# One run of row products a layer instead of four, in the gated recurrence of a decoder trunk

## The chip, the cores and the metric

The kernel runs on one core of a Trainium2 chip. The core has five engines with a queue each: TensorE (PE in the profile; PEld is its loading of weights), VectorE (DVE), ScalarE (ACT), GpSimd (POOL) and SyncE (SP). Data lie in SBUF, and matmuls write to PSUM banks of 128 x 512 numbers. The metric is the device time of one execution in microseconds. Three runs of the kernel before took 386.99, 387.08 and 389.15 us; the median is 387.08.

## What is computed

Two layers of a decoder trunk on 256 positions of width 1024. Each layer normalises x, projects it to 10 groups of 512 columns, feeds three branches (block-sparse attention, a gated recurrence and cross-attention to a memory of 256 tokens), gates their outputs, projects them back and adds x. The change touches the recurrence alone, in the reference:

```python
def step(state, inp):                      # chunks of 64 positions, 4 heads, key and value width 128
    qc, lfc, kc, vc = inp
    A = jnp.cumsum(lfc, axis=2)
    diff = A[:, :, :, None, :] - A[:, :, None, :, :]
    decay = jnp.exp(jnp.where(causal[:, :, None], diff, -jnp.inf))
    scores = jnp.einsum('bhtd,bhtsd,bhsd->bhts', qc, decay, kc)
    o = (jnp.einsum('bhts,bhsv->bhtv', scores, vc)
         + jnp.einsum('bhtd,bhdv->bhtv', qc * jnp.exp(A), state))
    A_end = A[:, :, -1:, :]
    state = (jnp.exp(A_end[:, :, 0, :])[..., None] * state
             + jnp.einsum('bhsd,bhsv->bhdv', kc * jnp.exp(A_end - A), vc))
    return state, o
```

A score of positions t and s is thus the sum over 128 key dimensions of q(t), k(s) and the product of the forget gates between s and t.

## The kernel before

**Projections.** Weights come in chunks of 128 x 1024 (60 chunks a layer, the counter is `st["c"]`). Each chunk is loaded by DMA into `wr`, rounded by ACT to a high half `wh` (L213) and DVE subtracts to get the low half `wl` (L227). PE multiplies high by high, high by low and low by high (L275, products of 128 x 512, some of 128 x 256). Three buffers each hold `wh` and `wl`. After some of these products the emitting code calls `slot`, which makes further chunks (`h_to`, `l_to`) and lets every active generator go one step.

**Generators.** The branches are Python generators (`g_hgrn` is the recurrence). A `yield 2` lets two steps pass, and so places the generator's next instructions further on among the projections. `room(what, n)` waits, while the program is emitted, until n tiles of a kind are free in a bookkeeping (`held`, `room_of`); `rel` gives one back. Side tiles (`sd`) are four PSUM banks.

**Order.** `schedule_with_timeline_sim=True` (L1499) lets a planner order the instructions of each engine along a simulated timeline. `keep_in_program_order` pins an instruction (`mm_row`, L278, does it for the row products), and `in_turn` writes an order out by hand. Hand-written orders cover the chunks up to 13 of layer 1 (L1318 to L1333) and, in both layers, those from 36 on (L1304 to L1316, L1335 to L1344); the recurrence lies between them, in chunks 16 to 31.

**The recurrence.** With keys on partitions, Q, K and F (forget gates) are 128 x 1024 tiles, one column a position and head. The decay between positions is built level by level, so that every score inside a block of 32 positions is a product of a Q column that carries some gates and a K column that carries others:

- level 1 (pairs): Q carries F (L896), then a row run (L899), then the pair's gate product hT1 (L901), hQ2 (L904) and K times F in place (L907);
- levels m = 2 and m = 8 (L911 to L954): Q columns (L919, L920), a row run (L924), gate products, the next Q tile (L947 to L949), and K of three of four groups times a gate, in place (L950);
- the carry at 32 (`carry`, L866) writes hQb and hKb, and a last run (L961 to L973) multiplies K and Q between blocks of 32 and of 64;
- the carry at 64 (L975) works in place, and hKb times hQb of whole heads follows (L991).

A row run (`row`, L880) is 32 products, eight by four, each with a 128 x 32 piece of K as weights and 48 columns of Q, into four 32-partition strips of one side tile. Each shows in the trace as two matmuls, so a run has 64. The masked copies (`keep`, L889, on DVE at L892) take from the side tile the parts that belong to this level into the block-diagonal tile hSd; two follow the first run and three each the next two. hSd and the last run's side tile are then copied into hST (L978, L983, on ACT). Much later the products of hST with the values follow (L1008).

Since K is changed in place, the K product of a level waits for the row run that reads it.

Of the kernel before, what the change touches and what calls it, by code (L numbers as in the profile page):

```python
# [12 lines left out]
F32 = mybir.dt.float32  # L13
# [5 lines left out]
OP = mybir.AluOpType  # L19
# [26 lines left out]
def hymba_kernel(ctx: ExitStack, tc: tile.TileContext, x, mem, mem_t, positions, w_in, w_out, w_mem_kv,  # L46
                 gains, moba_g, out):
    nc = tc.nc
# [15 lines left out]
    def room(what, n=1):  # L64
        while held[what] + n > room_of[what]:
            yield
# [14 lines left out]
    def rel(what="sd", n=1):  # L81
        held[what] -= n
# [696 lines left out]
    def pairs(a, n):  # L779
        return a.rearrange("p (n m) -> p n m", m=n)  # L780
# [76 lines left out]
    def g_hgrn(l):  # L857
# [8 lines left out]
        def carry(m, Tm, src, dst=None):  # L866
            (Qv, Kv), (Qo, Ko) = ([halves(a, m) for a in p] for p in (src, dst or src))
            n = 1024 // (2 * m)
            Tv = Tm.rearrange("p (n two) -> p n two", two=2)
            nc.vector.tensor_tensor(Qo[:, :, 1], Qv[:, :, 1], Tv[:, :, 0:1].to_broadcast([128, n, m]), op=OP.mult)  # L870
            nc.vector.tensor_tensor(Ko[:, :, 0], Kv[:, :, 0], Tv[:, :, 1:2].to_broadcast([128, n, m]), op=OP.mult)
            if dst is not None:
                nc.scalar.copy(Qo[:, :, 0], Qv[:, :, 0])
                nc.scalar.copy(Ko[:, :, 1], Kv[:, :, 1])
            if m < 64:
                T2 = sb.tile([128, n], F32, name=f"hT{m}", tag=f"hT{m}", bufs=1)
                nc.vector.tensor_tensor(T2, Tv[:, :, 0], Tv[:, :, 1], op=OP.mult)
                return T2

        def row(q, m):  # L880
            g = side_tile()
            for i in range(8):
                for j in range(4):
                    c = i * 4 + j
                    mm_row(g[j * 32:j * 32 + 32, i * 48:i * 48 + 48].rearrange("p (n m) -> p n m", m=m),
                           K[:, c * 32:c * 32 + 32], q(c))
            return g[:, :384].rearrange("p (a n m) -> p a n m", a=8, m=m)

        def keep(g, j, n, lo, hi):  # L889
            def part(a):  # L890
                return a.rearrange("p a (n m) -> p a n m", m=n)[:, :, :, lo:hi]
            nc.vector.copy_predicated(part(hSd), part(mk[:, j][:, None, :].to_broadcast([128, 8, 32])), g)  # L892


        F2, K2 = pairs(F, 2), pairs(K, 2)
        nc.vector.tensor_tensor(Q[:, :, 2], Q[:, :, 1], F2[:, :, 1], op=OP.mult)  # L896
        yield 2
        yield from room("sd")
        g = row(lambda c: Q[:, c * 16:c * 16 + 16], 3)  # L899
        Tm = sb.tile([128, 512], F32, name="hT1", tag="hT1", bufs=1)  # L900
        nc.vector.tensor_tensor(Tm, F2[:, :, 0], F2[:, :, 1], op=OP.mult)  # L901
        yield 2
# [1 line left out]
        nc.vector.tensor_tensor(n4[:, :, 0:4], Q[:, :, 0:3:2].rearrange("p (g a) i -> p g a i", a=4),  # L904
                                F2[:, :, 0].rearrange("p (g a) -> p g a", a=4)[:, :, :, None]
                                .to_broadcast([128, 128, 4, 2]), op=OP.mult)
        nc.vector.tensor_tensor(K2[:, :, 0], K2[:, :, 0], F2[:, :, 1], op=OP.mult)  # L907
        keep(g[:, :, :, 0:2], 0, 2, 0, 2)
        keep(g[:, :, :, 2:3], 1, 2, 1, 2)
        rel()  # L910
        for m in (2, 8):  # L911
            n = 256 // m
            q, T4, K4 = n4, pairs(Tm, 4), K.rearrange("p (g a i) -> p g a i", a=4, i=m)

            def by(j, w, k=None):
                return T4[:, :, j:j + w, None].to_broadcast([128, n, w, m]) if k is None else \
                    T4[:, :, j:j + 1, None].to_broadcast([128, n, k, m])
            yield
            nc.vector.tensor_tensor(q[:, :, 4:6], q[:, :, 2:4], by(1, 2), op=OP.mult)  # L919
            nc.vector.tensor_tensor(q[:, :, 6:7], q[:, :, 5:6], by(1, 1), op=OP.mult)  # L920
            yield 2
            yield from room("sd")
            b = 8 // m
            g = row(lambda c: q[:, c * b:c * b + b, 1:7].rearrange("p g a i -> p g (a i)") if b > 1  # L924
                    else q[:, c, 1:7].rearrange("p a i -> p (a i)")[:, None, :], 6 * m)
            nc.vector.tensor_tensor(T4[:, :, 2], T4[:, :, 2], T4[:, :, 3], op=OP.mult)
            nc.vector.tensor_tensor(T4[:, :, 1], T4[:, :, 1], T4[:, :, 2], op=OP.mult)
            Tn = sb.tile([128, n], F32, name=f"hT{m}", tag=f"hT{m}", bufs=1)
            nc.vector.tensor_tensor(Tn, T4[:, :, 0], T4[:, :, 1], op=OP.mult)
            yield 2  # L930
            if m == 2:
                n4 = sb.tile([128, 32, 7, 8], F32, name="hQ3", tag="PTh", bufs=1)

                def to(c, w):
                    return n4[:, :, 0:4].rearrange("p g a (c i) -> p g a c i", i=m)[:, :, :, c:c + w]

                def split(a):
                    return a.rearrange("p (g b) a i -> p g b a i", b=4)
            else:
                n4 = sb.tile([128, 1024], F32, name="hQ", tag="hq0", bufs=1)  # L940

                def to(c, w):
                    return n4.rearrange("p (g c i) -> p g c i", c=4, i=m)[:, :, c:c + w]

                def split(a):
                    return a
            nc.scalar.copy(to(0, 1), split(q[:, :, 0:1]))  # L947
            nc.vector.tensor_tensor(to(1, 1), split(q[:, :, 1:2]), split(by(0, 1)), op=OP.mult)
            nc.vector.tensor_tensor(to(2, 2), split(q[:, :, 4:7:2]), split(by(0, 1, 2)), op=OP.mult)  # L949
            nc.vector.tensor_tensor(K4[:, :, 0:3], K4[:, :, 0:3], by(1, 3), op=OP.mult)  # L950
            for k, (lo, hi, at) in enumerate(((1, 4, 0), (2, 4, 3), (3, 4, 5))):
                keep(g[:, :, :, at * m:(at + hi - lo) * m], (2 if m == 2 else 5) + k, 4 * m, lo * m, hi * m)
            rel()
            Tm = Tn  # L954
        base = n4, K
        other = [sb.tile([128, 1024], F32, name=n, tag=t, bufs=1) for n, t in (("hQb", "PTl"), ("hKb", "PTh"))]
        yield
        T2 = carry(32, Tm, base, other)
        yield 2
        yield from room("sd")  # L960
        g = side_tile()  # L961
        for a in range(0, 8, 2):
            for q in (0, 64):
# [4 lines left out]
        for a in range(0, 8, 2):  # L968
            for b in range(2):
                for q in (0, 32):  # L970
                    c = (a + b) * 128
                    mm_row(g[b * 64 + q:b * 64 + q + 32, 128 + a * 32:128 + a * 32 + 64],
                           other[1][:, c + q:c + q + 32], other[0][:, c + 64:c + 128])  # L973
        yield 2
        carry(64, T2, other)  # L975
        S2 = St.rearrange("p (a b) s -> p a b s", b=2)
        for q in range(0, 128, 32):
            nc.scalar.copy(St[q:q + 32, :, q:q + 32], hSd[q:q + 32])  # L978
# [10 lines left out]
        g = side_tile()  # L989
        for h in range(4):  # L990
            mm(g[:, h * 128:(h + 1) * 128], K4[:, h, 0:128], Q4[:, h, 128:256], True, True)  # L991
        rel("PTh")
        rel("PTl")
        xc = sb.tile([128, 512], F32, name="hX", tag="hX", bufs=1)
        nc.scalar.copy(xc, g)
        rel()
# [506 lines left out]
```

## Time and profile before

| | |
|---|---|
| median of three runs | 387.08 us |
| profiled execution | 387.04 us, span 385.3 us |
| granted PE clock | 0.999 |
| PE, PEld busy | 99%, 83% |
| DVE, ACT, POOL busy | 84%, 65%, 23% |
| matmuls that are row products or the last run's (L279, hQ with hK, hQb with hKb) | 448 + 64 |

How to read what is quoted. The page gives the busy time of each engine, and the chain of work that ended last, followed back from the last instruction. In the chain in order of time a line is start, length and the pieces merged into it. A list of waits has the engine and line that waited, who released it, the total, how often and the longest. A row of a timeline is start, length, engine, line, operation, output <- inputs, shape and count, with the idle time of the engine ahead of it and its releaser in brackets. Ends of matmuls are modelled and overlap, so their starts are what to go by. Tile names lose their trailing numbers: hQ stands for hQ1, hQ2, hQ3 and hQ.

### The profile page before, as it was taken

To read this page: it belongs to the slowest core of one execution; us is meant where nothing else is said; L and a number is where in the kernel's file an instruction comes from. 1 tells how busy PE (TensorE), PEld (TensorE's weight loads), DVE (VectorE), ACT (ScalarE), POOL (GpSimd) and SP (SyncE) were. 2 spreads that over 40 slices of the span, in tenths; PEclk is the share of its full clock that TensorE was granted. 3 is DMA by queue.
4 is the path that set the end of the run, shared out by engine and by line. 5 is a ranking of instruction groups with operands and counts; after the bars stand their busy time and mean duration, and the time that the engine had idled before them with its cause. 6 is when DMAs were issued, how large, how long until landed. Compare 5 with 4: busy or idle time off the path is not lost.

```text
span 385.3 us, 6801 instructions
## 1 busy us (share of the span) xinstructions
PE 379.6 (99%) x2447; PEld 318.9 (83%) x2447; DVE 322.9 (84%) x631; ACT 249.4 (65%) x422; POOL 89.4 (23%) x135
## 2 busy tenths in 40 slices
PE   7999999999999999999999999999999999999996
PEld 5888888788888888888888888888888888888885
DVE  4789799999679999967596989899698699798763
ACT  4988855567769749654366866445765985794540
POOL 3004400643202523220031030014062063134000
PEclk9999999999999999999999999999999999999999
DMA  7985595438534889875559667736756189898612
GB/s 255 421 323 186 177 315 198 149 128 277 215 109 159 273 272 354 317 259 169 162 168 299 200 210 236 255 111 184 253 193 194 54 277 269 318 325 264 202 39 109
DMA packets 26577, 85.53 MB, mean 222 GB/s; under 512 B 3632, under 2 KB 6064, under 8 KB 26544
## 3 DMA queue, kind: packets, MB, share of 16 engines
q1 hardware_dynamic: 22304, 71.31, 55.4%
q0 software_dynamic: 3952, 13.64, 11.3%
q8 instruction: 19, 0.31, 0.3%
q10 hardware_dynamic: 288, 0.15, 0.1%
q14 instruction: 14, 0.11, 0.1%
HBM read 75.13 MB, written 9.96 MB: 221 GB/s over the span
## 4 chain that ended last, share of the span: by engine, by line
PE 97%; DMA 1%; DVE 0%; SPq 0%; ACT 0%; issue 0%; DVEq 0%
PE acc L275 58%; PE acc L1361 17%; PE acc L310 11%; PE sd L275 5%; PE sd L279 4%; DMA wr<-in_w_mem_kv_dram 1%; PE sd L1071 0%; PE sd L1205 0%; PE sd L490 0%; PE acc L279 0%; PE sd L545 0%; SPq L177 0%; ACT wh L217 0%; DVE xs L1415 0%; DVE xs L1422 0%
## 5 line engine op out<-in xcount | busy, mean ns | idle before, releaser
L213 ACT CAST wh<-wr 128x1024 fp32r<-128x1024 f32 x96 | 100.8, 1051 | 58.0 <-PE acc L275 38.8
L227 DVE TENSOR_TENSOR wl<-wr,wh 128x1024 fp32r<-128x1024 f32 x96 | 117.1, 1222 | 22.6 <-ACT wh L213 20.4
L275 PE MATMUL acc<-wh,hT 128*128 128x512 f32 x384 | 123.1, 394 | 0.0
L275 PEld LDWEIGHTS acc<-wh,hT 128*128 128x128 f32 x384 | 71.5, 188 | 15.0 <-issue 0.7
L275 PE MATMUL acc<-wl,hT 128*128 128x512 f32 x192 | 75.6, 394 | 0.0
L275 PE MATMUL acc<-hT,wh 128*128 128x512 f32 x256 | 63.9, 392 | 0.0
L275 PEld LDWEIGHTS acc<-hT,wh 128*128 128x128 f32 x256 | 46.5, 189 | 8.5
L275 PEld LDWEIGHTS acc<-wl,hT 128*128 128x128 f32 x192 | 36.1, 188 | 7.3
L217 ACT ACTIVATE wh<-wr,gT 128x1024 fp32r<-128x1024 f32 (+1 forms) x29 | 28.9, 1011 | 13.1 <-DMA wr<-in_w_mem_kv_dram 5.9
L1361 PE MATMUL acc<-wl,yh 128*128 128x512 f32 (+1 forms) x96 | 37.2, 387 | 0.0
L1361 PE MATMUL acc<-wh,yl 128*128 128x512 f32 (+1 forms) x96 | 37.1, 387 | 0.0
L275 PEld LDWEIGHTS acc<-hT,wl 128*128 128x128 f32 x256 | 34.8, 190 | 2.2
L231 DVE SCALAR_TENSOR_TENSOR wl<-wr,gT,wh 128x1024 fp32r<-128x1024 f32 (+1 forms) x29 | 31.1, 1096 | 6.1 <-ACT wh L217 6.1
L275 PE MATMUL acc<-hT,wl 128*128 128x256 f32 x256 | 35.7, 282 | 0.0
L1361 PE MATMUL acc<-wh,yh 128*128 128x512 f32 (+1 forms) x96 | 30.6, 390 | 0.0
L310 PE MATMUL acc<-wh,mTh 128*128 128x512 f32 x64 | 25.4, 400 | 1.0 <-ACT wh L217 0.7
L1036 POOL TENSOR_TENSOR rka<-msa,pw 128x8 f32<-128x8 f32 x4 | 12.1, 3022 | 59.2 <-DVE msa L1035 59.2
L310 PE MATMUL acc<-wh,mTl 128*128 128x512 f32 x64 | 24.8, 390 | 0.0
L1116 ACT ACTIVATE P<-P,nba,rq 128x128 f32<-128x128 f32 (+1 forms) x32 | 17.1, 536 | 7.0 <-DVE nba L1110 7.0
L1361 PEld LDWEIGHTS acc<-wh,yl 128*128 128x128 f32 x96 | 18.0, 188 | 3.7
L1361 PEld LDWEIGHTS acc<-wl,yh 128*128 128x128 f32 x96 | 18.0, 188 | 3.6
L1361 PEld LDWEIGHTS acc<-wh,yh 128*128 128x128 f32 x96 | 17.7, 188 | 3.6 <-issue 0.3
(233 smaller groups left out, 591.3 us busy)
## 6 DMA issues: line engine op xcount, KB each, us to landing
wr<-in_w_in_dram SPq DMA_DIRECT2D x80, 512.0 KB, 4.2
wr<-in_w_out_dram SPq DMA_DIRECT2D x24, 512.0 KB, 4.9
wr<-in_w_mem_kv_dram SPq DMA_DIRECT2D x15, 512.0 KB, 5.2
there<-blk POOLq DMA_DIRECT2D x7, 512.0 KB, 4.8
there<-blk POOLq DMA_DIRECT2D x4, 768.0 KB, 6.3
PT<-there POOLq DMA_DIRECT2D x16, 192.0 KB, 5.7
there<-blk SPq DMA_DIRECT2D x4, 512.0 KB, 2.9
P<-there POOLq DMA_DIRECT2D x16, 128.0 KB, 3.9
```

Source lines behind the costliest of these rows:

```text
L213: N["wh", i] = nc.scalar.copy(whs[i], raws[i])
L217: N["wh", i] = nc.scalar.activation(whs[i][:, sl], raws[i][:, sl], AF.Copy, scale=gT[:, g:g + 1])
L227: N["wl", i] = nc.vector.tensor_tensor(wls[i], raws[i], whs[i].bitcast(F32), op=OP.subtract)
L231: ins = nc.vector.scalar_tensor_tensor(wls[i][:, sl], in0=raws[i][:, sl], scalar=gT[:, g:g + 1], in1=whs[i][:, sl].bitcast(F32), op0=OP.mu ...
L275: nc.tensor.matmul(o, lhsT=a, rhs=b, start=s, stop=e)
L279: tc.keep_in_program_order(nc.tensor.matmul(o, lhsT=a, rhs=b, start=s, stop=e))
L310: N["kv", i, g, t, j] = nc.tensor.matmul(acc[g][t], lhsT=x[:, c, ts], rhs=y, start=c == 0 and j == 0, stop=c == 7 and j == 2)
L1036: nc.gpsimd.tensor_tensor(r[:, t8], ms[:, t8], pw[:, :8], op=OP.pow)
L1116: N["exp", u, c] = nc.scalar.activation(P[:, i, kc[t]], P[:, i, kc[t]], AF.Exp, bias=nb[:, c:c + 1], scale=rq[:, r:r + 1], accum_out=sm[:, ...
L1361: ins = nc.tensor.matmul(a, lhsT=y, rhs=wt[:, cs], start=n == (0 if to is None else nk - 2) and j == 0, stop=n == nk - 1 and j == 2)
```

## The change

The row products of levels 1, 2 and 8 are no longer issued when their Q and K columns are ready. Each level puts its K tile, a function that cuts its Q columns and a width on a list, and all three runs are issued ahead of the last run, once four side tiles are free, so that 128 products stand together. For that, what they read has to stay until then: K after levels 1, 2 and 8 is written to a tile of its own each time (hK1, hK2, hK8, in buffers of tiles that are idle there), with the part that isn't multiplied copied by ACT; hQ3 moves to a buffer of P, and hQb and hKb to those of the recurrence's output y. The buffers PTh and PTl are given back right behind the run. The eight masked copies follow the second carry.

```diff
--- before.py
+++ after.py
@@ -877,7 +877,9 @@
                 nc.vector.tensor_tensor(T2, Tv[:, :, 0], Tv[:, :, 1], op=OP.mult)
                 return T2
 
-        def row(q, m):
+        rows = []
+
+        def row(K, q, m):
             g = side_tile()
             for i in range(8):
                 for j in range(4):
@@ -894,9 +896,8 @@
 
         F2, K2 = pairs(F, 2), pairs(K, 2)
         nc.vector.tensor_tensor(Q[:, :, 2], Q[:, :, 1], F2[:, :, 1], op=OP.mult)
+        rows.append((K, lambda c: Q[:, c * 16:c * 16 + 16], 3))
         yield 2
-        yield from room("sd")
-        g = row(lambda c: Q[:, c * 16:c * 16 + 16], 3)
         Tm = sb.tile([128, 512], F32, name="hT1", tag="hT1", bufs=1)
         nc.vector.tensor_tensor(Tm, F2[:, :, 0], F2[:, :, 1], op=OP.mult)
         yield 2
@@ -904,32 +905,32 @@
         nc.vector.tensor_tensor(n4[:, :, 0:4], Q[:, :, 0:3:2].rearrange("p (g a) i -> p g a i", a=4),
                                 F2[:, :, 0].rearrange("p (g a) -> p g a", a=4)[:, :, :, None]
                                 .to_broadcast([128, 128, 4, 2]), op=OP.mult)
-        nc.vector.tensor_tensor(K2[:, :, 0], K2[:, :, 0], F2[:, :, 1], op=OP.mult)
-        keep(g[:, :, :, 0:2], 0, 2, 0, 2)
-        keep(g[:, :, :, 2:3], 1, 2, 1, 2)
-        rel()
+        K = sb.tile([128, 1024], F32, name="hK1", tag="yh0", bufs=1)
+        nc.scalar.copy(pairs(K, 2)[:, :, 1], K2[:, :, 1])
+        nc.vector.tensor_tensor(pairs(K, 2)[:, :, 0], K2[:, :, 0], F2[:, :, 1], op=OP.mult)
+        yield from room("P")
+        held["P"] += 1
         for m in (2, 8):
             n = 256 // m
             q, T4, K4 = n4, pairs(Tm, 4), K.rearrange("p (g a i) -> p g a i", a=4, i=m)
 
-            def by(j, w, k=None):
+            def by(j, w, k=None, T4=T4, n=n, m=m):
                 return T4[:, :, j:j + w, None].to_broadcast([128, n, w, m]) if k is None else \
                     T4[:, :, j:j + 1, None].to_broadcast([128, n, k, m])
             yield
             nc.vector.tensor_tensor(q[:, :, 4:6], q[:, :, 2:4], by(1, 2), op=OP.mult)
             nc.vector.tensor_tensor(q[:, :, 6:7], q[:, :, 5:6], by(1, 1), op=OP.mult)
             yield 2
-            yield from room("sd")
             b = 8 // m
-            g = row(lambda c: q[:, c * b:c * b + b, 1:7].rearrange("p g a i -> p g (a i)") if b > 1
-                    else q[:, c, 1:7].rearrange("p a i -> p (a i)")[:, None, :], 6 * m)
+            rows.append((K, (lambda c, q=q, b=b: q[:, c * b:c * b + b, 1:7].rearrange("p g a i -> p g (a i)")) if b > 1
+                         else (lambda c, q=q: q[:, c, 1:7].rearrange("p a i -> p (a i)")[:, None, :]), 6 * m))
             nc.vector.tensor_tensor(T4[:, :, 2], T4[:, :, 2], T4[:, :, 3], op=OP.mult)
             nc.vector.tensor_tensor(T4[:, :, 1], T4[:, :, 1], T4[:, :, 2], op=OP.mult)
             Tn = sb.tile([128, n], F32, name=f"hT{m}", tag=f"hT{m}", bufs=1)
             nc.vector.tensor_tensor(Tn, T4[:, :, 0], T4[:, :, 1], op=OP.mult)
             yield 2
             if m == 2:
-                n4 = sb.tile([128, 32, 7, 8], F32, name="hQ3", tag="PTh", bufs=1)
+                n4 = sb.tile([128, 32, 7, 8], F32, name="hQ3", tag="P", bufs=2)
 
                 def to(c, w):
                     return n4[:, :, 0:4].rearrange("p g a (c i) -> p g a c i", i=m)[:, :, :, c:c + w]
@@ -947,17 +948,18 @@
             nc.scalar.copy(to(0, 1), split(q[:, :, 0:1]))
             nc.vector.tensor_tensor(to(1, 1), split(q[:, :, 1:2]), split(by(0, 1)), op=OP.mult)
             nc.vector.tensor_tensor(to(2, 2), split(q[:, :, 4:7:2]), split(by(0, 1, 2)), op=OP.mult)
-            nc.vector.tensor_tensor(K4[:, :, 0:3], K4[:, :, 0:3], by(1, 3), op=OP.mult)
-            for k, (lo, hi, at) in enumerate(((1, 4, 0), (2, 4, 3), (3, 4, 5))):
-                keep(g[:, :, :, at * m:(at + hi - lo) * m], (2 if m == 2 else 5) + k, 4 * m, lo * m, hi * m)
-            rel()
+            K = sb.tile([128, 1024], F32, name=f"hK{m}", tag={2: "hF", 8: "yl0"}[m], bufs=1)
+            Kn = K.rearrange("p (g a i) -> p g a i", a=4, i=m)
+            nc.scalar.copy(Kn[:, :, 3], K4[:, :, 3])
+            nc.vector.tensor_tensor(Kn[:, :, 0:3], K4[:, :, 0:3], by(1, 3), op=OP.mult)
             Tm = Tn
         base = n4, K
-        other = [sb.tile([128, 1024], F32, name=n, tag=t, bufs=1) for n, t in (("hQb", "PTl"), ("hKb", "PTh"))]
+        other = [sb.tile([128, 1024], F32, name=n, tag=t, bufs=1) for n, t in (("hQb", "yh1"), ("hKb", "yl1"))]
         yield
         T2 = carry(32, Tm, base, other)
         yield 2
-        yield from room("sd")
+        yield from room("sd", 4)
+        gs = [row(*r) for r in rows]
         g = side_tile()
         for a in range(0, 8, 2):
             for q in (0, 64):
@@ -971,8 +973,18 @@
                     c = (a + b) * 128
                     mm_row(g[b * 64 + q:b * 64 + q + 32, 128 + a * 32:128 + a * 32 + 64],
                            other[1][:, c + q:c + q + 32], other[0][:, c + 64:c + 128])
+        rel("P")
+        rel("PTh")
+        rel("PTl")
         yield 2
         carry(64, T2, other)
+        keep(gs[0][:, :, :, 0:2], 0, 2, 0, 2)
+        keep(gs[0][:, :, :, 2:3], 1, 2, 1, 2)
+        rel()
+        for m, f in ((2, gs[1]), (8, gs[2])):
+            for k, (lo, hi, at) in enumerate(((1, 4, 0), (2, 4, 3), (3, 4, 5))):
+                keep(f[:, :, :, at * m:(at + hi - lo) * m], (2 if m == 2 else 5) + k, 4 * m, lo * m, hi * m)
+            rel()
         S2 = St.rearrange("p (a b) s -> p a b s", b=2)
         for q in range(0, 128, 32):
             nc.scalar.copy(St[q:q + 32, :, q:q + 32], hSd[q:q + 32])
@@ -989,8 +1001,6 @@
         g = side_tile()
         for h in range(4):
             mm(g[:, h * 128:(h + 1) * 128], K4[:, h, 0:128], Q4[:, h, 128:256], True, True)
-        rel("PTh")
-        rel("PTl")
         xc = sb.tile([128, 512], F32, name="hX", tag="hX", bufs=1)
         nc.scalar.copy(xc, g)
         rel()
```

## The prediction

> **What bounds the kernel now.** I read the page first: the span, the busy shares and the chain that ended last.
>
> ```profile
> span 385.3 us, 6801 instructions
> PE 379.6 (99%) x2447; PEld 318.9 (83%) x2447; DVE 322.9 (84%) x631; ACT 249.4 (65%) x422; POOL 89.4 (23%) x135
> PE 97%; DMA 1%; DVE 0%; SPq 0%; ACT 0%; issue 0%; DVEq 0%
> ```
>
> TensorE (PE) is busy 99% of the span, and 97% of the chain that sets the end is PE work. A busy share says little by itself, so the second view is the list of waits of PE: everything it ever waited for.
>
> ```profile
> PE sd L275 <- DVE dm L405: 1.0, 1, 1.0
> PE acc L310 <- ACT wh L217: 0.7, 1, 0.7
> PE acc L310 <- ACT mTh L431: 0.3, 1, 0.3
> ```
>
> All three belong to the start (warm-up and memory weights). From the first weight tile on, PE has no wait at all. So the time is the sum of what PE executes; a change moves it only if it changes that sum or makes PE wait. The profiled execution took 387.04 us for its span of 385.3, so 1.7 us lie around the span; the median of the runs is 387.08. I work against 387.04.
>
> The third view is the chain in order of time, in the stretch of layer 0 with the recurrence's row products (sd L279), then three pieces of the same stretch of layer 1.
>
> ```profile
> 55.84 5.44 PE acc L275 x24
> 61.28 0.82 PE sd L279 x64
> 62.10 6.34 PE acc L275 x27
> 68.44 0.82 PE sd L279 x64
> 69.26 7.25 PE acc L275 x31
> 76.50 0.82 PE sd L279 x64
> 77.32 7.48 PE acc L275 x32
> 84.80 0.88 PE sd L279 x63
> 85.68 6.58 PE acc L275 x28
> 92.25 0.89 PE sd L275 x8
> ...
> 255.98 7.93 PE acc L275 x34
> 263.90 0.82 PE sd L279 x64
> ...
> 272.43 0.88 PE sd L279 x63
> ```
>
> Columns are start, length and what ran. A run of 32 row products shows as 64 matmuls. Four such runs stand among the projections of each layer, each some 7 us after the last.
>
> **What a run costs, and what joining saves.** An undisturbed projection product costs 5.44 / 24 = 0.2267 us (first row). The 27 behind the first run took 6.34 us where 27 x 0.2267 = 6.12: 0.22 us went into leaving that run and entering the next. The other stretches give the same: 7.25 - 31 x 0.2267 = 0.22, 7.48 - 32 x 0.2267 = 0.23, and in layer 1 7.93 - 34 x 0.2267 = 0.22. So a run takes 0.82 + 0.22 = 1.04 us out of the projections' time. What do the 64 matmuls cost when no edge is counted? Two looks into the first run, cut at different instants, both starting with its first matmul:
>
> ```profile
> 61.21 0.49 PE L279 MATMUL sd<-hQ,hK 128*32 128x48 f32 x26
> 61.21 0.84 PE L279 MATMUL sd<-hQ,hK 128*32 128x48 f32 x60
> ```
>
> 34 more matmuls cost 0.35 us, 10.3 ns each; 64 of them 0.66 us. A run in one piece with its neighbour therefore saves 1.04 - 0.66 = 0.38 us; allowing for rounding I take 0.36. The change keeps all 128 products of a layer and turns four runs into one: three joins a layer, six in all, 6 x 0.36 = **2.2 us**. A seam inside the joined run changes the K tile, the Q tile and the PSUM bank. The nearest row is the fourth run, which already has such a seam (hQ with hK, then hQb with hKb, and wider products): 0.88 us against 0.82, so a seam costs at most 0.06, six of them 0.36; the lower bound is nothing, and I take nothing, since its second half also has wider products to explain the 0.06.
>
> The Trainium skill (TensorEngine Tiling (Array Packing), Key Properties) says that changing the tiling mode drains TensorE, and TensorE: Matmul & The Clock Gate (Single matmul latency) puts the part of a warm matmul that a stream hides at about 166 ns. An estimate by those two, two drains for each join removed, is 0.33 us, and the sum 2.0; the trace's 0.36 is used.
>
> **The parts that are not on PE, and who pays.** The row products no longer run level by level, so the copies that keep their blocks (L892) move behind the joined run, and the K product of a level writes a new tile instead of its source; ScalarE (ACT) copies the untouched part. VectorE (DVE) is the engine to look at, since it also makes the low half of each weight tile (L227).
>
> ```profile
> 61.00:84.00 23.00, 23.00 (x282) 18.58 (x281) 22.35 (x62) 13.01 (x18) 10.49 (x18) 1.00 0.50 165
> 248.00:272.00 24.00, 24.00 (x285) 19.48 (x285) 23.80 (x50) 12.45 (x16) 5.73 (x2) 1.00 0.53 175
> ```
>
> This table of stretches has length, then PE, weight loads, DVE, ACT, POOL, the granted clock (1.00), DMA share and GB/s. DVE is busy 22.35 of 23 us and 23.80 of 24 us between the first and the last run: as full as PE, and kept off the critical chain only by weight tiles made ahead. ACT is about half free.
>
> ACT's new copies: one of 128x512 and two of 128x256 a layer. The larger form costs 0.62 us here, and the smaller no more:
>
> ```profile
> 73.58 0.62 ACT L873 COPY hQb<-hQ 128x512 f32<-128x512 f32 x1 [1.42 <-DVE hQ L949]
> ```
>
> That is at most 1.9 us a layer on an engine with 10 us free in that stretch: costed at nothing. If that cover were gone, the weight casts (L213) would come that much later, and at worst 3.8 us in all would reach PE.
>
> The wait that the change adds: the joined run stands where the fourth run stood in PE's order and needs the first carry's output, hKb (L871), as that one did. It gets there earlier, because three runs of 1.04 us no longer precede it. What of DVE's work before L871 goes? The masked copies:
>
> ```profile
> L892 DVE COPY_PREDICATED hSd<-mk,sd 128x128 f32<-128x128 uint8 (+3 forms) x8 | 2.9, 365 | 0.0
> ```
>
> ```profile
> 64.34 0.47 DVE L892 COPY_PREDICATED hSd<-mk,sd 128x256 f32<-128x256 uint8 x1
> 64.67 0.45 DVE L948 TENSOR_TENSOR hQ<-hQ,hT 128x256 f32<-128x256 f32 x1
> ...
> 82.51 0.68 DVE L871 TENSOR_TENSOR hKb<-hK,hT 128x512 f32<-128x512 f32 x1
> ...
> 269.95 0.68 DVE L871 TENSOR_TENSOR hKb<-hK,hT 128x512 f32<-128x512 f32 x1
> ```
>
> Eight copies last 2.9 us, but the next instruction starts 0.33 us after a copy of 0.47, so they hold DVE for about 0.7 x 2.9 = 2.0 us. In DVE's order six of the eight stand ahead of L871: 1.5 us. Layer 0: hKb is complete at 82.51 + 0.68 - 1.5 = 81.7, PE reaches the run at 84.80 - 3 x 1.04 = 81.7. Layer 1: 269.95 + 0.68 - 1.5 = 269.1, against 272.43 - 3.12 = 269.3. A dead heat in one layer, 0.2 us to spare in the other. Behind the run in PE's order stand projections that need nothing of it, and all of them would wait. The bounds: no wait at all (the K products no longer wait for the row run that read their source, so the planner may place them sooner), or, if none of the 1.5 us comes forward, 1.5 + 1.3 = 2.8 us in both layers. I take 0.1 a layer, near the lower end, because the rows above put the two within 0.2.
>
> After the run, the K Q product (92.25 in the chain) takes a side tile that the first masked copies must have released; the run (81.7 + 2.9), the second carry (two products of 0.68) and two copies are over by 87, and 92.25 - 3 x 0.36 is 91.2. If that cover were gone, PE would wait for the difference. The tiles newly held until the run (the buffers of P, PTh, PTl) are asked for next by the attention, later than the run. Nothing on the SP and POOL queues is moved, and no DMA is added.
>
> Sum: 387.04 - 2.2 + 0.2 = **385.0 us**.
>
> **Rivals.** *A. DVE becomes the bound of the stretch.* PE would pass the 61 to 84 stretch in 23 - 3.1 = 19.9 us, while DVE has 22.35 - 1.5 = 20.9 us in it; in layer 1 the pair is 20.9 and 22.3. If all of that work were due before the run, PE would wait 1.0 + 1.4 = 2.4 us, and the time would be 387.2. For it: the full DVE column. Against: weight tiles made ahead, and DVE work of other branches that can be done later. Halfway, 386.1, is the likely size where this happens.
>
> *B. The copies block ACT (slower).* The copies of the diagonal blocks into hST (L978) now need all eight masked copies, which come after the joined run.
>
> ```profile
> 273.26 1.65 ACT L978 COPY hST<-hSd 32x256 f32<-32x256 f32 x4 [2.19 <-DVE hSd L892]
> 274.93 1.82 ACT L983 COPY hST<-sd 32x128 f32<-32x128 f32 x6
> 276.78 1.05 ACT L213 CAST wh<-wr 128x1024 fp32r<-128x1024 f32 x1
> ...
> 277.86 1.23 DVE L227 TENSOR_TENSOR wl<-wr,wh 128x1024 fp32r<-128x1024 f32 x1 [3.23 <-ACT wh L213]
> ...
> 280.39 0.39 PE L275 MATMUL acc<-wl,hT 128*128 128x512 f32 x1
> ```
>
> Already now ACT stood 2.19 us at L978, a weight cast waited behind it, DVE waited 3.23 us for that cast, and its low half, ready at 279.09, was used at 280.39: 1.3 us to spare. In the changed kernel the run ends near 272.2; the second carry (two products of 0.68) and eight copies (2.0 us) put L978 at 275.6; L978 and L983 take 3.5, the cast 1.05, the low half 1.23: 281.4, where PE wants it at 280.39 - 1.1 = 279.3. PE would wait 2.1 us in layer 1, and about as much in layer 0: 387.04 - 2.2 + 4.2 = 389.0. It decides from the point where L978 keeps its place ahead of that cast and starts over 0.2 us later than now. Against it: the planner orders engines by a simulated timeline (L1499), in which the cast is ready before L978. The Trainium skill (TensorE: Matmul & The Clock Gate, engine queue depth) speaks for this rival: ScalarE and VectorE take their queues strictly in order, so a cast cannot pass a waiting copy; the trace agrees, with the 2.19 us above and the cast behind them.
>
> *C. The change doesn't do what it says.* Projections fall between the rows of the joined run, since only the rows are pinned: with one such cut a layer two of three joins remain, 387.04 - 1.4 = 385.6. Against: the fourth run's two emissions show as one piece of 63.
>
> **Chances.** Forecast (384.6 to 385.4) 0.50; A 0.24; B 0.13; C 0.05; better than 384.6, by other waits that happen to go or a cheaper edge, 0.05; something worse than 391, a reordering that starves PE in several places, 0.03. The range 384.5 to 387.5 holds the forecast, A, C and a little of the two ends, about 0.82. Less than 1%, 3.9 us, can hardly be told from no change here. Faster by over 1% needs nearly twice the sum of all joins: 0.02. Slower by over 1% needs more than B's price: 0.04. Within 1%: 0.94.
>
> **What would show it.** In the chain of the changed kernel: one piece of sd L279 a layer, about 255 matmuls in 0.88 + 3 x 0.66 = 2.9 us, with 0.22 us of edge in the projections around it; the L870 and L871 of the first carry ending before it starts. A would show as PE (or its weight loads) waiting for wl L227 or hKb L871 between 64 and 84 us or 250 and 272; B as PE waiting for wh or wl shortly after the run, and ACT idle at L978; C as more than two pieces of row products. The forecast is wrong if the time is above 386 with no new wait of PE: then edges cost less than I worked out.

## The result, and the profile after

The change makes the kernel slower. Six runs of it took 392.94 us in the median (390.04 to 394.80), six runs of the kernel before on the same chip 387.11 (386.80 to 389.15); the ratio is 1.0144 with a 95% interval of 1.0112 to 1.0176. The prediction of 385.0 us has the wrong sign, and the time lies 5.4 us above its range. The profiled execution took 392.76 us, its span 391.0.

The page of the changed kernel, the lines that answer to those shown of before, and the one that counts PE's instruction transfers:

```profile
span 391.0 us, 6806 instructions
PE 380.2 (97%) x2447; PEld 319.8 (82%) x2447; DVE 323.9 (83%) x631; ACT 252.4 (65%) x428; POOL 89.2 (23%) x135
q8 instruction: 19, 0.31, 0.3%
PE 95%; DMA 2%; issue 1%; SPq 0%; DVE 0%; ACT 0%; DVEq 0%
```

PE has the same 2447 matmuls and only 0.6 us more of busy time, but the span is 5.7 us longer: the time went into PE standing still. The list of PE's waits says where, and that nobody released it:

```profile
PE sd L279 <- issue: 5.4, 2, 3.5
PE sd L275 <- DVE dm L405: 1.0, 1, 1.0
PE acc L310 <- ACT wh L217: 0.4, 2, 0.2
PE acc L310 <- ACT mTh L431: 0.2, 1, 0.2
```

The last three lines name the waits of the start that the kernel before has too, with a little less time. The first is new: two waits of the row products, 5.4 us together, released by "issue", which is the profile's word for time in which an engine waits for nothing that is recorded. The chain in order of time shows them inside the joined runs, one in each layer:

```profile
80.09 2.47 PE sd L279 x221
82.56 1.90 issue
84.46 0.65 PE sd L279 x31
...
267.85 1.82 PE sd L279 x155
269.67 3.51 issue
273.18 0.90 PE sd L279 x66
274.07 7.07 PE acc L275 x23
281.14 0.58 PE sd L279 x32
```

Two more things are to be seen here. The 23 projection products behind the second gap took 7.07 us, where 23 x 0.2267 = 5.21 and an edge of 0.22 would be 5.43. And in layer 1 the last 32 row matmuls stand apart, at 281.14. The table of stretches (columns as in the prediction) shows what the clock and the DMA did:

```profile
82.50:84.40 1.90, 0.08 (x6) 0.00 (x0) 1.90 (x4) 0.00 (x0) 0.90 (x1) 1.00 0.00 0
...
269.70:273.20 3.50, 0.03 (x4) 0.03 (x4) 3.50 (x7) 0.62 (x1) 0.00 (x0) 1.00 0.90 291
273.20:278.00 4.80, 4.80 (x80) 3.92 (x81) 2.79 (x8) 0.00 (x0) 0.00 (x0) 0.64 0.58 168
```

In the first gap the DMA was idle, in the second it was busy at 0.90. Behind the second gap the granted clock was 0.64 in the mean of 4.8 us; behind the first it stayed at 1.00.

To see what each place costs I cut the span at three starts in PE's timeline: the first projection product, and the first product of keys and queries of the attention (kT with qT) in each layer, which stands at the end of the layer's projections of x. Each stretch holds the same number of matmuls in all kernels of the table, but for tiny products that some of them add to the warm-up, in the first column. The rows are profiled executions; the four columns add up to the span.

| kernel | up to the first projection | layer 0 to kT.qT | on to layer 1's kT.qT | rest |
|---|---|---|---|---|
| before | 30.15 | 74.78 | 186.97 | 93.36 |
| after | 29.79 | 76.17 | 191.64 | 93.38 |
| rows at their own level | 29.08 | 75.08 | 187.11 | 93.34 |
| joined in twos | 31.08 | 75.28 | 186.63 | 94.13 |
| after, 64 instructions ahead | 32.17 | 76.66 | 186.80 | 93.38 |
| after, 176 ahead | 30.62 | 74.72 | 192.87 | 93.37 |
| joined in layer 1 alone | 30.12 | 75.05 | 186.26 | 93.37 |
| after again | 30.11 | 76.19 | 192.75 | 93.37 |
| joined in twos again | 29.80 | 75.12 | 186.63 | 94.13 |
| joined in twos, less set-up | 31.43 | 74.37 | 186.62 | 94.14 |
| before, 64 instructions ahead | 29.95 | 75.77 | 186.97 | 93.36 |
| joined in layer 1, layer 0 as before | 29.76 | 75.87 | 186.27 | 93.38 |

So the changed kernel loses 1.39 us in layer 0 and 4.67 in layer 1, and the rest is as it was.

### The profile page after: what moved, and what is told of

Same layout as the page of the kernel before. It is cut to its first block, busy times and chain, and to the rows that moved or that the text cites. A ratio compares the mean times of both kernels' runs of the same rounds, so it can differ in the third digit from the quotient of the medians.

```text
span 391.0 us, 6806 instructions
## 1 busy us (share of the span) xinstructions
PE 380.2 (97%) x2447; PEld 319.8 (82%) x2447; DVE 323.9 (83%) x631; ACT 252.4 (65%) x428; POOL 89.2 (23%) x135
## 4 chain that ended last, share of the span: by engine, by line
PE 95%; DMA 2%; issue 1%; SPq 0%; DVE 0%; ACT 0%; DVEq 0%
PE acc L275 57%; PE acc L1371 17%; PE acc L310 11%; PE sd L275 5%; PE sd L279 4%; DMA wr<-in_w_mem_kv_dram 2%; PE sd L1081 0%; PE sd L490 0%; PE sd L1215 0%; PE acc L279 0%; SPq L177 0%; PE sd L545 0%; ACT wh L217 0%; DVE xs L1425 0%; DVE xs L1432 0%
## 5 line engine op out<-in xcount | busy, mean ns | idle before, releaser
L227 DVE TENSOR_TENSOR wl<-wr,wh 128x1024 fp32r<-128x1024 f32 x96 | 117.0, 1220 | 25.2 <-ACT wh L213 23.2
L275 PEld LDWEIGHTS acc<-wh,hT 128*128 128x128 f32 x384 | 72.3, 190 | 15.8 <-issue 0.7
```

Of the source, the lines that this page charges most:

```text
L227: N["wl", i] = nc.vector.tensor_tensor(wls[i], raws[i], whs[i].bitcast(F32), op=OP.subtract)
L275: nc.tensor.matmul(o, lhsT=a, rhs=b, start=s, stop=e)
```

## The experiments

**The theory** (F in the expectations). PE ran out of instructions. The page counts 19 transfers of 0.31 MB on PE's instruction queue, 16 KB each. A joined run of 128 row products is 256 matmuls and 256 weight loads, 512 instructions, and PE takes 256 of them in 128 x 10.3 ns = 1.3 us, where projections take 256 instructions in 128 x 0.2267 = 29 us. Counted in the trace's records, PE stopped at its instruction 1216 in layer 0 and at 3520 in layer 1: 2304 apart, 9 x 256. During each stop exactly one block landed. The DMA view of the changed kernel, cut to 81.8:83.2 and then to 269.7:273.2 us (packets, MB, share):

```profile
q8 instruction: 1, 0.02, 5.7%
```

```profile
q8 instruction: 1, 0.02, 1.7%
```

**The rivals.** A missing input (a K tile, a side tile, the copies on ACT) that the records don't show (D); or something in a long run of small products as such, whatever stands around it (S). These give a stop at the same product of the run however the program around it is shifted, and the first goes away with the moved tiles and copies.

### Each row run at its own level again

```diff
-        rows.append((K, <Q columns>, width))
+        yield from room("sd")
+        gs.append(row(K, <Q columns>, width))      # at each of the three levels
...
-        yield from room("sd", 4)
-        gs = [row(*r) for r in rows]
+        yield from room("sd")
```

> Everything of the change but the join: K tiles of their own, the moved buffers, the ACT copies and the eight masked copies behind the second carry stay; each row run is issued at its own level again, as in the kernel before. Theory F (PE runs out of instructions: they come in blocks of 256, a joined run uses up 256 in 1.35 us, and the next block needs 3.6 to 6 us): four runs of 128 instructions a layer lie 6 to 8 us apart, no gap of PE inside a run, time 386.5 to 387.6. Rival D (PE waits in the run for data: the new K tiles, the carry, the moved copies, by a wait that the profile doesn't show): the gaps stay, in the last runs or near them, 390 or more.

Measured: 387.01 us against 386.65, ratio 1.0002 (0.9981 to 1.0022), and no wait of PE in a row run in its list. (At one seam, in the last run of layer 1, PE went on 0.21 us after the product before it, and 0.06 us after DVE had finished hKb.) All moved tiles, ACT copies and late masked copies are still in it. They are thus not what costs the 5.7 us; the joining is.

### Joined in twos

```diff
+            if m == 2:
+                yield from room("sd", 2)
+                gs = [row(*r) for r in rows]
...
-        yield from room("sd", 4)
-        gs = [row(*r) for r in rows]
+        yield from room("sd", 2)
+        gs.append(row(*rows[2]))
```

> All of the change, but the runs of levels 1 and 2 are joined at the place of the second run, and that of level 8 is joined with the last run: two runs of 256 instructions a layer instead of one of 512. Theory F: a run of 256 holds no whole block of 256 between two projections, so no gap; three joins are left (in layer 1 the planner sets the hQb part of the last run apart), 3 x 0.36 = 1.1 us less than before: 385.7 to 386.4. Rival D: the gaps stay at the last run, 389 or more. Rival S (any dense stretch of row products slows PE down, in proportion to its length): half the loss of the changed kernel, about 390.

Measured: 387.36 us, ratio 1.0013 (0.9991 to 1.0035). No gap inside a run, as the theory asks of 256 instructions in a row. But the gain that was expected did not come: the time should have been below before's. The table has the pieces: layer 1 is 0.34 us shorter, one join; layer 0 is 0.50 longer and the rest 0.77 longer. The chain shows the latter in the attention of layer 1, where the planner now puts two projection products, which stood behind it before, into the run of kT with qT. The 24, 8 and 12 products of that place take 5.81 us in the kernel before (from 291.96 to 297.77) and 6.59 here:

```profile
295.01 0.42 PE acc L279 x2
295.44 0.66 PE acc L275 x2
296.10 1.06 PE acc L279 x6
```

And layer 0 has a wait of PE for an accumulator that ACT had not yet copied:

```profile
77.55 0.50 PE L275 MATMUL acc<-wh,hT 128*128 128x512 f32 x1 [0.49 <-ACT ih L797]
```

```profile
75.44 0.62 ACT L874 COPY hKb<-hK 128x512 f32<-128x512 f32 x1 [0.94 <-DVE rt L601]
...
76.92 0.58 ACT L797 COPY ih<-acc 128x512 f32<-128x512 f32 x1
```

ACT stood 0.94 us at the copy of hKb, waiting for DVE, and the copy that frees the accumulator stands behind it in ACT's order. Weight loads of PE also waited 0.5 us for a low half (wl, L227).

### Before, with three unread runs ahead of the last one

```diff
-        yield from room("sd")
+        yield from room("sd", 4)
+        for _ in range(3):
+            row(<48 of the Q columns of base[0]>, 3)
+        rel("sd", 3)
```

> The kernel before, its data flow untouched, with three row runs more whose results nobody reads, right ahead of the last run of each layer, reading what the last run reads anyway; so the last run is a piece of 512 instructions, as in the changed kernel. The products alone cost 6 x 0.66 = 4.0 us: 391.1. Theory F: a gap of 2 to 4 us inside the long run of layer 0, after about 153 of its 256 matmuls, and one of 0 to 1 us in layer 1, where the fetch is asked for some 32 instructions ahead of the run; with a slower clock behind the gap, 393 to 396. Rival D: no gap, 391.1.

The kernel before gets a run of 128 products out of rows that nobody reads. Its chain in layer 0 and in layer 1:

```profile
84.27 1.82 PE sd L279 x154
86.08 1.61 issue
87.69 1.39 PE sd L279 x97
...
275.86 2.95 PE sd L279 x251
```

A gap after 154 matmuls in layer 0, where the count of instructions put it at 153, and none in layer 1. So the gap needs nothing of the change but the run's length, and the same run stops in one place and not in another. One run took 392.56 us: six more runs of 0.66 and the gap of 1.8 make 5.8 on top of before.

### The changed kernel with 64 instructions more ahead

```diff
         mm(pt[:, :256], zb[:, :128], zb, True, True)
+    for _ in range(32):
+        mm(pt[:, :16], zb[:, :128], zb[:, :16], True, True)
     rel()
```

> The changed kernel with 32 tiny matmuls (64 instructions) more in the warm-up, where PE waits for the first weights anyway; nothing else changes but the number of instructions ahead of everything. Theory F: the gap keeps its place in the count of instructions. In layer 0 it comes 32 matmuls earlier in the run, after about 192 instead of 225, still 1.5 to 3 us. In layer 1 no whole block lies inside the run any more (boundaries fall about 123 matmuls into the run and behind its end), so the gap of 3.5 us and the slow clock after it go: 387 to 389.5. Rivals D and S: the gaps stay at the same products in both layers, time that of the changed kernel, 390 to 395.

The 32 tiny products stand in the warm-up, before any data is there. The chain in layer 0 and layer 1:

```profile
83.22 2.18 PE sd L279 x192
85.39 1.66 issue
...
271.26 2.47 PE sd L279 x223
273.73 5.44 PE acc L275 x23
```

In layer 0 the stop came after 192 matmuls instead of 225: 64 instructions earlier in the run, give or take one product, and so at the same place in the program's count. In layer 1 it is gone, and with it the slow clock. Time 388.05 us, ratio 1.0028 (1.0004 to 1.0052); the profiled execution, 390.79 us, has a start 2.0 us longer than before's and a wait of 0.8 us for `ih` in layer 0. In layer 1 the trace has the products of PE and the work of DVE and ACT in the same order as without the shift; in layer 0 the planner exchanged a few instructions. Both rivals fall here: neither a missing input nor the run's own nature knows of 64 instructions executed in the warm-up.

### 176 instructions ahead

The same edit with `range(88)`.

> The changed kernel with 88 tiny warm-up matmuls (176 instructions) more ahead of everything. Theory F (the gap belongs to the count of instructions): now layer 0 is the lucky one. A boundary falls some 16 instructions into its run, the block after it was asked for about 5 us ahead of the run, and the next boundary lies behind the run: no gap inside the run, or one under 0.7 us. In layer 1 a boundary falls about 67 matmuls into the run, so the gap is back, after about 195 of the run's 224 matmuls, 2 to 4 us, with a slow clock after it. Rivals D and S: gaps as in the changed kernel, in both layers.

```profile
80.86 1.61 PE sd L279 x137
82.47 0.51 issue
82.98 1.54 PE sd L279 x115
...
267.24 2.42 PE sd L279 x195
269.66 3.73 issue
273.39 0.64 PE sd L279 x23
```

The stops moved to 137 and 195 matmuls, the latter as counted beforehand. In layer 0 the gap is only 0.5 us. One run took 393.37 us.

### Layer 1's weights not loaded

```diff
+            if 60 + 24 <= i < 60 + 36:
+                raws[i] = raws[i - 1]
+                st["dma"] += 1
+                continue                             # chunks 84 to 95: no DMA
...
-            yield from across(o.rearrange("p (q r) -> p q r", q=4), flat, 8)
+            yield from across(o.rearrange("p (q r) -> p q r", q=4), flat, 8, pace=(2 + 4 * l, 4))
```

> The changed kernel without the weight loads of layer 1 around its run: chunks 84 to 95 are computed with the weights of chunk 83, so the result is another; and the transfer that turns the attention's K is issued four steps later. Theory F with queueing (the fetch stands behind weight and turning transfers in the DMA engines): the gap of layer 1 shrinks from 3.5 to about 1.9 us, which layer 0 shows, where the DMA engines are nearly idle. Theory F with a fixed latency: it stays between 3 and 4 us. Layer 0 is unchanged.

If the block that PE waits for stands behind the weights in the DMA engines, the gap of layer 1 shrinks when they go. The stretch of the gap, and the chain:

```profile
269.70:273.20 3.50, 1.92 (x160) 1.78 (x163) 3.50 (x5) 1.67 (x2) 0.00 (x0) 1.00 0.39 153
```

```profile
269.74 1.82 PE sd L283 x155
271.55 1.58 issue
273.13 0.90 PE sd L283 x65
274.03 5.44 PE acc L279 x23
```

The stop is at the same instruction; it shrank from 3.5 us to 1.6, and the clock behind it stayed up (5.44 us for the 23 products that took 7.07). Layer 0, unchanged, had 2.3 us this time instead of 1.9, with a clock of 0.50 behind it; so one place varies by half a us between executions, and the drop in layer 1 is well beyond that. The total of this one run, 392.82 us, says nothing: a new wait of 1.6 us for the memory attention's mP came in later.

### The changed kernel again

> The changed kernel once more beside the kernel before on this chip. Theory F: gaps at the same two instructions as in its first profile (after 225 and 155 matmuls of the runs), with lengths that differ by up to 1 us since the fetch is a transfer among others; 390 to 394. If a data wait were the cause, the gaps would move with the data and not sit on the same instruction.

In a later set of runs: 394.09 us against 386.75, ratio 1.0203 (1.0180 to 1.0226). The waits:

```profile
PE sd L279 <- issue: 5.6, 2, 3.8
```

They are at the same two instructions, 1216 and 3520, and again the clock fell behind the longer one.

**Where the gap falls, and how long it is.** Counted in instructions from the start of a joined run, a block boundary (every 256th) lies at these places:

| run | boundaries inside | stop at | gap, us from start to start |
|---|---|---|---|
| after, layer 0 | 192, 448 | 448 | 2.09 |
| after, layer 1 | 52, 308 | 308 | 3.71 |
| unread rows, layer 0 | 50, 306 | 306 | 1.81 |
| unread rows, layer 1 | 28, 284 | none | - |
| 64 ahead, layer 0 | 127, 383 | 383 | 1.87 |
| 64 ahead, layer 1 | 242 | none | - |
| 176 ahead, layer 0 | 16, 272 | 272 | 0.72 |
| 176 ahead, layer 1 | 132, 388 | 388 | 3.93 |
| weights not loaded, layer 0 | 192, 448 | 448 | 2.49 |
| weights not loaded, layer 1 | 52, 308 | 308 | 1.79 |
| after again, layer 0 | 192, 448 | 448 | 1.98 |
| after again, layer 1 | 52, 308 | 308 | 4.01 |
| joined in twos, all | one at most | none | - |

PE never stops at the first boundary of a run. It stops at the second, shortly or not at all where the first stands within 30 instructions of the run's start. Read as a supply: two blocks are at hand, PE works in one while the next is complete, and reaching the boundary between them sets off the transfer of the block after both. The single records of the instruction queue in the traces, ten transfers at ten stops, fit that but for one. From PE's crossing of the first boundary the next block's transfer started 0.7 to 1.4 us later where the DMA was idle or the weights were left out, and 2.9 to 3.2 us later behind weights; it took 0.9 to 1.3 us, and PE went on 1.3 to 1.5 us after it landed. Together that is 3.2 to 3.8 us and 5.1 to 5.5 us, against the 1.3 to 1.6 us that these 256 instructions of row products last; the differences are the gaps. The short gap of 0.72 is the exception: its transfer was under way 1.4 us before PE came to the boundary, 16 instructions into the run. Among projections that is common: in the kernel before, the transfers at 43.36 and 70.27 us started 2.8 and 4.5 us, or 33 and 38 recorded instructions, before PE came to the boundary. So what asks for a block seems to run some tens of instructions ahead of what PE executes, and a boundary that lies close behind the start of a run is passed while the projections still last. That, and that two blocks are held, is my reading of these times; the traces do not show the buffer itself. The Trainium skill (Runtime: NRT & Kernel Launch, Instruction fetch mechanics) states blocks of 256 instructions fetched while the current one runs, and calls the cost of a boundary mostly hidden. The size agrees with 2304 = 9 x 256; that it is hidden holds here for projections, and not for 512 row instructions in a row.

### Joined in layer 1 alone, 64 ahead

```diff
+    for _ in range(32):                              # in the warm-up
+        mm(pt[:, :16], zb[:, :128], zb[:, :16], True, True)
...
+            if l == 0:
+                yield from room("sd")
+                gs.append(row(*rows[-1]))            # at each level
...
+        if l:
+            gs = [row(*r) for r in rows]
```

> The join in layer 1 alone, with the 64 extra instructions that let its run pass without a gap; in layer 0 each row run stands at its own level. Theory F: no gap in either layer. Two joins are left (the planner sets the hQb part of layer 1 apart): 2 x 0.36 = 0.7 us less than before, ratio about 0.998. Rival A (VectorE, as full as PE, takes the gain back) was seen with two joined pairs in layer 0, where PE waited about 1 us for low weight halves; if it holds in layer 1 too, the ratio is 1.000 or above and PE shows waits for wl there.

```profile
267.07 2.47 PE sd L279 x223
269.54 5.44 PE acc L275 x23
274.98 0.58 PE sd L279 x32
```

386.48 us against 386.75, ratio 0.9987 (0.9973 to 1.0001). No gap. The stretch of layer 1 is 186.26 against 186.97: 0.71 us for two joins (the last 32 matmuls are still apart), 0.36 each, as the prediction priced an edge. Layer 0 is 0.27 longer with no run joined. The wait that the expectation takes from the joined pairs is, in their trace, half for a low half (0.5 us of the weight loads) and half for `ih` (0.5 us).

### Joined in twos, with DVE relieved

```diff
-        periods(0, 22, 0.0)                          # range reduction of the rotary angles,
-        take(0, 22, 0, 1)                            # and the rest of it
...
+            nc.vector.tensor_copy(rt[:, 6 + q], an)
```

> The kernel with two joined pairs a layer, without the range reduction of the rotary angles (some 30 small VectorE instructions in the recurrence's stretch of layer 0), so the rotary factors are others. Theory A0 (VectorE is as full as PE in layer 0, and with the joined pairs it delays the copies that ScalarE has ahead of the accumulators' copy, ih, and of the casts, until PE waits): the waits of PE for ih and low halves near 76 to 80 us go, and the time is 0.5 to 1.2 us below the same kernel with the reduction. If the joined pairs lose their gain elsewhere, the two are equal within 0.3 us.

This was run beside the joining in twos once more:

> The two joined pairs a layer once more, on the same chip as the kernel without the angle reduction: 386.8 to 387.6, no gap inside a run, and in layer 0 PE waits of 0.5 to 1.0 us for ih and low halves.

Measured: 386.48 us without the range reduction, 0.9993 (0.9979 to 1.0007), and 387.34 with it, 1.0013 (0.9997 to 1.0029), both against 386.73. Layer 0 took 74.37 and 75.12 us (before 74.78). In the second the starts of PE's projection products show 0.58 us lost at the one that waits for `ih` and 0.39 at one that waits for a low half; in the first both are gone, and 0.26 us at the seam of the last run, where hKb came late, are new. With two joins of 0.36 that gives 0.25 above and 0.46 below the layer 0 of before; measured are 0.34 above and 0.41 below. So what was missing in layer 0 is DVE's work coming late, to PE itself and through ACT's order. The 0.77 us in the attention of layer 1 stayed in both.

### Before, with 64 instructions ahead

The same 32 tiny products in the kernel before.

> The kernel before with the 64 extra warm-up instructions alone, as a control: four short runs a layer hold no whole block of instructions wherever the boundaries fall, and the extra matmuls lie in PE's wait for the first weights. Theory F: no gap, ratio 0.998 to 1.002. If it is faster by as much as the kernel with the join in layer 1 alone, that kernel's gain is not the join's.

387.00 us against 386.73, ratio 1.0003 (0.9987 to 1.0018), and no gap in a row run: what the shift did to the changed kernel it does not do to the kernel before.

### Layer 0 as before, layer 1 joined, 64 ahead

```diff
+    def g_hgrn_by_level(l):                          # the recurrence of the kernel before
...
-            spawn(g_hgrn(l))
+            spawn(g_hgrn(l) if l else g_hgrn_by_level(l))
```

> Layer 0 exactly as in the kernel before (K in place, each run at its level), layer 1 as in the changed kernel, with the 64 extra warm-up instructions that keep a whole block of instructions out of its run. Theory F with the edge price: no gap inside the run of layer 1, its stretch 0.72 us shorter for two joins, layer 0 unchanged: 386.0, ratio 0.998. If the moved tiles themselves cost nothing in layer 0, this equals the kernel with the join in layer 1 alone and moved tiles in both layers (0.9987).

```profile
267.51 2.47 PE sd L279 x223
269.99 5.45 PE acc L275 x23
275.44 0.58 PE sd L279 x32
```

386.43 us against 386.95 in the medians, 0.13% less; the ratio is 0.9976 (0.9957 to 0.9995), the only interval of all versions that lies below 1, if barely. The firmer evidence is layer 1, which is 0.70 us shorter, two joins again. Its profiled execution had a wait of 1.0 us for `ih` in layer 0, and the one of the control above 0.9. In both, ACT had stood 2.3 to 2.4 us for the DMA of a weight chunk near 59 us, which the trace of before does not have; that this is the cause was not tested.

## Why the prediction was wrong, point by point

**The step that failed** is the price of the joined run: 128 products at 64 x 10.3 ns a run, plus a seam between nothing and 0.06. It took that pace from 64 matmuls and carried it to 256, on the ground that PE "has no wait at all" and that its work is the sum of what it executes. The pace itself held: the 128 matmuls between the first boundary and the stop took 1.33 us in layer 0 and 1.40 in layer 1, 10.4 and 10.9 ns each. What the sum left out is PE's supply of instructions. I went through DVE, ACT, side tiles and queues as things that PE could come to wait for, and not through PE's own program, though the page's row of instruction transfers stood in the profile before as well, word for word. The upper bound of a seam was read from a run of 64 matmuls, 128 instructions, which cannot reach a second block boundary. But the trace of before could have raised the question: its 19 block transfers took 0.9 to 1.8 us each, and a block of row products lasts 1.3.

The sum with that term, for the two profiles. Layer 1: gap by starts 3.71, less two joins 0.71, plus the slow clock behind it, 7.07 - 5.44 = 1.63: 4.63, measured 4.67. Layer 0: gap 2.09, less three joins 1.08, plus 0.30 of a wait that follows below: 1.31, measured 1.39.

**The edge, 0.36 us a join:** right. In layer 1 it was 0.71 and 0.70 for two joins, 0.34 and 0.35 for one.

**One piece of about 255 matmuls:** in layer 0, with the gap in it. In layer 1 the planner set 32 aside, so two of three joins were made there: rival C, with 0.05, held in one layer.

**The dead heat at hKb:** too dark in layer 0, where hKb was complete by 77.9 (L871 started at 77.2) and the run began at 80.0; PE did not wait for it. In layer 1 L871 started at 273.00, 5.2 us after the run's first matmul, and the planner had set apart the products that need hKb. In two of the experiments PE did wait for hKb, 0.21 us (rows at their own level, layer 1) and 0.26 (joined in twos, less set-up, layer 0), so such a wait is real there, if small.

**ACT's new copies at nothing:** nearly. In layer 0 a copy stood 0.49 us for DVE, and the copy of `ih` behind it came late:

```profile
72.93 0.62 ACT L873 COPY hQb<-hQ 128x512 f32<-128x512 f32 x1 [0.49 <-DVE hQ L950]
73.46 0.58 ACT L797 COPY ih<-acc 128x512 f32<-128x512 f32 x1
```

```profile
73.68 0.92 PE L275 MATMUL acc<-wh,hT 128*128 128x512 f32 x2
...
74.43 0.40 PE L275 MATMUL acc<-wl,hT 128*128 128x512 f32 x1
```

Two products from 73.68 to 74.43, 0.75 us where 0.45 is normal: PE waited 0.30 us for its accumulator. The kernel with each row at its level shows 0.26 at the same product, and is 0.30 longer in layer 0. So this belongs to the moved tiles and copies, and it is what rivals A and B described, DVE late and ACT in strict order, at another place and at a tenth of their price.

**Rival A** (2.4 us of DVE) **and rival B** (weight casts behind L978): not seen in the changed kernel. ACT did stand for 8.3 us ahead of a cast near 278, but because PE, which had to free the buffer, stood itself.

**The chances:** slower by over 1% had 0.04, for "more than B's price" of reorderings. It came about by one mechanism that none of the cases named, at two places.

## What to carry to other kernels

A run of small matmuls is limited by more than its products: each row product here brings four instructions, and a run that eats a block of 256 faster than the next can be fetched (here 1.3 us against 3.2 us and more) stops, with "issue" as the only releaser. When runs are joined, count the instructions and keep the joined piece to about one block, or see where the block boundaries lie: here a run of 448 instructions passed without a stop where only one boundary lay in it, and a few instructions put in long before decided that. Put a resource on the list of bounds before it has ever been short; and where a stop of PE is long enough to pull the clock down, its price is the gap plus what runs slowly behind it.

## What the runs showed of the hardware that was not expected

- PE's instruction supply can stop it: 0.7 to 4.0 us, always at a block boundary in the program's count (1216, 1472, 3520, 3776; each a multiple of 256 apart), never at the first boundary of a run.
- The block's transfer shares the DMA engines with the weights: the gap in layer 1 was 3.71 us at a DMA share of 0.90 and 1.79 us with the weights left out (share 0.39), in one run.
- The clock fell after gaps of 3.71, 3.93, 4.01 and 2.49 us, and stayed up after those of 2.09, 1.98, 1.87, 1.81, 1.79 and 0.72. The traces give the granted clock in stretches whose lengths, but for the last, are multiples of 3.41 us (in the changed kernel 269.65 at 1.00, 3.41 at 0.50, from 274.5 on, and 112.64 at 1.00). Cut into pieces of 3.41 us from those instants, PE stood idle for 2.1 to 2.4 us in the piece ahead of each fall, and for at most 1.7 us in any piece of the gaps without one. So the place of a gap counts with its length: the one of 2.49 us had 2.2 idle us in one piece, the one of 2.09 us was split into 0.8 and 1.1. This is worked out from ten gaps. The Trainium skill (TensorE: Matmul & The Clock Gate, What's actually happening) gives an idle window of about 3.4 us for the fall; the length of the pieces agrees, but here 2.1 idle us in one were enough.
- The slow clock is part of the spread of the changed kernel: the one run of the six with a mean granted clock of 1.000 took 390.04 us, the five others, at 0.990 to 0.995, took 391.33 to 394.80.
- What 64 instructions in the warm-up do to a kernel depends on its runs: nothing that can be measured in the kernel before (1.0003), and more than 1% in the changed one (1.0203 and 1.0144 without, 1.0028 with them), because they move the block boundaries.
